# A hybrid decoder layer on one core: the out-projection's weight sums moved to GpSimd's DMA queue, the input projection's sums spread over half blocks

## The chip, the cores and the metric

The kernel runs on one core of one Trainium2 chip. The metric is device time in microseconds (us) of one execution. A core has five engines with a queue each: TensorE (PE; its weight loads are PEld), VectorE (DVE), ScalarE (ACT), GpSimd (POOL) and SyncE (SP, which here only issues DMAs). An engine works through its queue in order. DMAs are issued from SP, from ACT and, after the change, from GpSimd. L12 is line 12 of the kernel before.

## What is computed

One layer of a decoder: a norm, one input projection, three token mixers, one output projection, a residual, a final norm. Cut to that:

```python
h = rms_norm(x, norm_w)
proj = h @ w_in                     # 528 tokens x 2048, all heads of all mixers
o_dn  = gated_delta_rule_chunked(q, k, v, log_a, beta) # 6 heads x 128, gate z
o_gla = gla_chunked(q, k, v, log_g)                    # 5 heads, gate z
o_fox = forgetting_attention(q, k, v, log_f)           # 5 heads x 128, gate z
o = concat([o_dn, o_gla, o_fox])
out = rms_norm(x + o @ w_out)
```

All in fp32, with 512 tokens of sequence and 16 learned ones ahead of them.

## The kernel before, in words

**Products.** Each fp32 operand is split into two parts: `hi`, a rounded copy made by ScalarE (L155), and `lo`, the rest, subtracted by VectorE (L156). A product is three matmuls (hi x hi, hi x lo, lo x hi). The input projection goes by blocks of 128 columns, in two half blocks of weights, each a DMA of 128x1024 on SP into `raw`, one of two buffers (`load_half`, L145), then the split into `whi` and `wlo`, then matmuls into banks `pp`. A load waits until the half block two before it has been split.

**Order of the work.** Delta-rule heads in two groups of three (`g` = 0 and 1): blocks for keys, values and queries, then a matrix inverse that runs mostly on VectorE (`dn_inverse`), whose result TensorE takes up in `pm` (L739), then the chunk recurrence (`dn_mix`). Then five gated-linear heads, five forgetting-attention heads (`fox_head`, numbered 0 to 4, from about 590 to 890 us), and the output projection from about 840 us on. A scheduler that simulates the timeline orders the instructions of each engine, so the projection's matmuls of one head stand between the attention of the head before. Scores (`pfa`, `pfd`) need k scaled by `rstd` on GpSimd (L1117), the transposes `pvf` need v scaled there (L1125), and the gate needs z scaled there (L1127).

**Products saved by sums.** Two places use fewer block products (Strassen's form), and need sums of weights. Both keep the sums in DRAM and read them back as weights.

- *Pairs of the input projection* (`in_sums`, L421): from head 1's v and z on, two blocks are projected together (`inproj_pair`; matmuls L516, casts and splits of halves of 512 columns, loads L504). For each of seven pairs there are four loads of 128x512 (L427, tile `is`), four subtractions or additions on VectorE (L429) and four stores to `ti` (L428), all DMAs on SP. Each sum is tied (`paced`) behind the split that was issued last.
- *The output projection* (`weight_sums`, L588): for each of four pairs of heads `j` and two halves, four loads of 128x512 (L593) into the thirds of one tile `ws`, four subtractions on VectorE (L595), four stores to `tw` (L594). The fourth load writes into a third that the second store reads, so it waits for that store's landing. The tile is one of eight buffers (`six`) which the attention uses too.

**Where the sums are called.** `AHEAD` names the sums that are called at a place of the main loop, `SUMS` those inside `fox_head(h)` behind its projection. Pairs 0 to 2 are called behind the keys, values and queries of group 0, pairs 3 to 6 behind the keys, values, queries and the inverse of group 1. Eight calls of `weight_sums(j, half)` lie in heads 1 to 3.

Of the kernel before, what the change touches and what calls it, by code (L numbers as in the profile page):

```python
# [83 lines left out]
def tile_hybrid_trunk(ctx, tc, xT, xtok, mtok, w_gate, w_in, w_out, w_dn, consts, lmask, fin_w, out, dbg=None):  # L84
    nc = tc.nc
# [13 lines left out]
    def row(name, dt=F32):  # L99
        return wk.tile([P, 3 + T], dt, tag="row", bufs=7, name=name)  # L100
# [44 lines left out]
    def load_half(src, name):  # L145
        raw = wp.tile([P, 1024], F32, tag="raw", name=f"raw{name}")
        nc.sync.dma_start(out=raw, in_=src)
        hi = wp.tile([P, 1024], F32R, tag="hi", name=f"whi{name}")
        lo = wp.tile([P, 1024], F32R, tag="lo", name=f"wlo{name}")
        split(raw, hi, lo)  # L150
        return hi, lo

    def split(raw, hi, lo):
        with tc.high_priority(offset=1000000):
            pace[0] = A.copy(hi, raw).ins  # L155
            pace[1] = V.tensor_tensor(out=lo, in0=raw, in1=hi.bitcast(F32), op=ALU.subtract).ins  # L156
# [3 lines left out]
    def paced(*ins):  # L160

        for x in ins:
            tc.add_manual_dep(x.ins, pace[x.ins.engine == pace[1].engine].name, mybir.DependencyInfo(
                mybir.DependencyClass.NoSync, mybir.DependencyReason.DATA), reason="paced")
# [11 lines left out]
    def part(name, n=512):  # L176
        return hp.tile([P, T], F32R, tag="x", name=name)[:, :n]
# [48 lines left out]
    def inproj(key, meta=True, first=0):  # L226
        if key not in done:
            b, ps, parts = inproj_begin(key, meta, first)
            head[key] = len(order)
            for half in range(2):  # L230
                inproj_part(ps, parts, 8 * half, 8, *load_half(w_in[b, half], f"{b}_{half}"))
            done[key] = [(p_[:, :n], t0, n) for p_, (t0, n) in zip(ps, parts)]
        return done.pop(key)
# [61 lines left out]
    for b in range(5):  # L295
        r = NM if b == 4 else P
        for c in range(2):
            t = wp.tile([P, 1024], F32, tag=("raw", "hi", "lo")[(2 * b + c) % 3], name=f"xt{b}{c}")
# [7 lines left out]
    for b in range(5):  # L306
# [3 lines left out]
        o = pr[1][:, :NM] if b == 4 else pr[0][:, b * P : (b + 1) * P]  # L310
# [24 lines left out]
    def silu(dst, src, name):  # L335
        n = src.shape[-1]
        t = row(f"st{name}")[:, :T]
        t = t[:, :n]
        G.tensor_scalar_max(t, src, LOW)  # L339
        A.activation(t, t, AF.Exp, scale=-1.0)  # L340
        A.activation(t, t, AF.Ln, bias=1.0)
        A.activation(t, t, AF.Exp, scale=-1.0)
        V.tensor_tensor(out=dst, in0=src, in1=t, op=ALU.mult)
# [3 lines left out]
    def gate_z(kind, h, t=None):  # L347
        parts = inproj((kind, h), meta=False)
        p_, t0, n = parts[0]
        z = row(f"z{kind}{h}")[:, :T]  # L350
        V.tensor_tensor(out=z[:, :S], in0=p_, in1=rstd[:, t0 : t0 + n], op=ALU.mult)  # L351
        if t is None:
            t = zp.tile([P, T], F32, tag="zs", name=f"zs{kind}{h}")[:, :S]
        silu(t, z[:, :S], f"{kind}{h}")
        zs[kind, h] = t
# [65 lines left out]
    def stage(name):  # L421
        return [zp.tile([P, T], F32, tag="zs", name=f"{name}{i}")[:, :512] for i in range(3)]

    def in_sums(n):
        h, one, two = PAIRS[n]
        x, y, z = stage(f"is{n}")
        get = lambda o, key, half: nc.sync.dma_start(out=o, in_=w_in[BLOCK_OF[key, h], half][:, :KC])  # L427
        put = lambda i, t: nc.sync.dma_start(out=ti[n][:, i], in_=t)  # L428
        two_ = lambda o, a, b, op: paced(V.tensor_tensor(out=o, in0=a, in1=b, op=op))  # L429
        get(x, two, 0)  # L430
        get(y, two, 1)
        get(z, one, 0)
        two_(y, x, y, ALU.add)
        two_(x, z, x, ALU.subtract)
        put(0, y)
        two_(z, y, z, ALU.subtract)
        put(2, x)
        put(1, z)
        get(x, one, 1)
        two_(x, x, z, ALU.subtract)  # L440
        put(3, x)

# [29 lines left out]
    def x_last(last):  # L472

        f = lambda u: u[:, HT:].bitcast(F32)
        for k in range(NK):
            if not last:
                if k % 2 == 0:
                    t = row(f"xe{k}")
                xr[k] = a = t[:, HT * (k % 2) : HT * (k % 2) + HT]
                V.tensor_tensor(out=a, in0=f(xh[k + 8]), in1=f(xh[k]), op=ALU.subtract)  # L480
                V.tensor_tensor(out=a, in0=a, in1=f(xl[k + 8]), op=ALU.add)
                V.tensor_tensor(out=a, in0=a, in1=f(xl[k]), op=ALU.subtract)
            else:
                A.copy(xh[k][:, HT:], xr[k])
                V.tensor_tensor(out=xl[k][:, HT:], in0=xr[k], in1=f(xh[k]), op=ALU.subtract)
# [101 lines left out]
    tw = drp.tile([SH // 2, 4, P, 1024], F32, name="tw")  # L587

    def weight_sums(j, half):
        c = slice(512 * half, 512 * half + 512)  # L590
        w = six.tile([P, 3, 512], F32, tag="six", name=f"ws{j}{half}")
        x, y, z = (w[:, i] for i in range(3))
        get = lambda o, i, J: nc.sync.dma_start(out=o, in_=w_dn[J, 2 * j + i][:, c])  # L593
        put = lambda n, t: nc.sync.dma_start(out=tw[j, n][:, c], in_=t)  # L594
        sub = lambda o, a, b: V.tensor_tensor(out=o, in0=a, in1=b, op=ALU.subtract)  # L595
        get(x, 0, 1)
        get(y, 0, 0)
        get(z, 1, 1)
        sub(y, x, y)
        sub(x, z, x)  # L600
        sub(z, z, y)
        put(0, y)
        put(2, x)
        put(1, z)
        get(x, 1, 0)
        sub(x, x, z)
        put(3, x)
# [175 lines left out]
    def dn_values(g, st):  # L783
        vp = six.tile([P, NN, P], F32, tag="six", name=f"vp{g}")
        vpm = t15(f"vpm{g}", (NM, H, P))
        br = st["br"]
        for j in range(H):
            h = H * g + j
            v = row(f"v{h}")[:, :T]
            conv_silu(("dv", h), 12 + h, v)  # L790
            pv = psm.tile([P, 512], F32, tag="m", name=f"pv{h}")
            for b in range(NB):
                PE.transpose(pv[:, b * P : (b + 1) * P], v[:, bsl(b)], ident)
            for b in range(NB):
                V.tensor_scalar_mul(vp[:, b * H + j, :], pv[:, b * P : (b + 1) * P], br[:, b, j : j + 1])
            pv2 = psm.tile([P, 512], F32, tag="m", name=f"pvm{h}")
            PE.transpose(pv2[:NM, :P], v[:, 0:NM], ident)
            V.tensor_scalar_mul(vpm[:, j, :], pv2[:NM, :P], br[:NM, 4, j : j + 1])
        st.update(vp=vp, vpm=vpm)

    def dn_queries(g, st):
        qT = six.tile([P, H, T], F32, tag="six", name=f"qT{g}")
        for j in range(H):
            conv_silu(("dq", H * g + j), H * g + j, qT[:, j], meta=False)
        st["qT"] = qT
# [273 lines left out]
    def fox_head(h):  # L1079
# [64 lines left out]
        if h == H1 - 1:  # L1144
            x_sums(XSUM.get(9, ()))
            x_last(False)
        if h in SUMS:
            for j, half in SUMS[h]:
                weight_sums(j, half)
# [47 lines left out]
        V.tensor_tensor(out=z, in0=po[:, :512], in1=z, op=ALU.mult)  # L1197


    SUMS = {1:[(0,1)],2:[(1,1),(3,0)],3:[(2,1),(3,1)]}  # L1200
    XLAST = 0
    AHEAD = {(0,0):(0,),(0,1):(1,),(0,2):(2,),(1,0):(3,),(1,1):(4,),(1,2):(5,),(1,3):(6,),("f",1):((0,0),),("f",2):((1,0),),("f",3):((2,0),)}
    XSUM = {1: (0,), 2: (1,2), 9:(3,)}
    PM = (308, 319)

    def ahead(g, i):
        for n in AHEAD.get((g, i), ()):
            weight_sums(*n) if isinstance(n, tuple) else in_sums(n)

    for g in range(2):  # L1210
        for h in range(max(NF, H * g), H * g + H):
            gate_z("dz", h)
        st = dn_keys(g)
        ahead(g, 0)
        dn_values(g, st)
        ahead(g, 1)
        dn_queries(g, st)
        ahead(g, 2)
        dn_inverse(g, st)
        ahead(g, 3)  # L1220
        dn_mix(g, st)
        for h in range(H * g, H * g + H):
            nc.sync.dma_start(out=zd[h], in_=zs["dz", h])
    for h in range(GLA_HEADS):
        gate_z("gz", h)
    for h in range(DN_HEADS):
# [22 lines left out]
    for mm, n in later:  # L1249
        n = head[n[0]] + n[1] if isinstance(n, tuple) else n  # L1250
        tc.add_manual_dep(mm, order[n].name, mybir.DependencyInfo(
            mybir.DependencyClass.NoSync, mybir.DependencyReason.DATA), reason="behind")


    for i in range(SH):
# [154 lines left out]
    for c in range(4):  # L1410
        f = part(f"fw{c}").bitcast(F32)
# [20 lines left out]
    for tb in range(4):  # L1432
        cuts = 2 if tb == 3 else 1
        for n in range(cuts):
            c = slice(512 // cuts * n, 512 // cuts * (n + 1))
# [79 lines left out]
```

## Time and profile before

| | us |
|---|---|
| median of 3 runs (1021.37 to 1025.98) | 1022.04 |
| the profiled execution | 1020.76 |
| its span, first to last instruction | 1019.0 |
| TensorE busy | 992.3 |
| VectorE busy | 674.8 |
| ScalarE busy | 460.9 |
| GpSimd busy | 195.2 |

The span is shorter than the execution's own time by what lies around it. The granted clock of TensorE is 0.996 over the span. The views name a group of instructions by line, engine, operation and tile (`out<-in`); a wait is read "who <- for whom: us in total, times, longest". A line of the view by stretches has the length, then busy us and (in brackets) the number of instructions of PE, PEld, DVE, ACT and POOL, the granted clock, the DMA engines' busy share and GB/s. Matmuls are pipelined and their ends are modelled, so busy TensorE isn't TensorE at its peak.

### The profile page before, as it was taken

The numbers are of one execution on the slowest core, as the hardware profiler recorded it, in microseconds if no ns is written. First come the engines' busy times: TensorE is split into PE (matmuls) and PEld (weight loads), VectorE is DVE, ScalarE is ACT, GpSimd is POOL, SyncE is SP. The second block draws the span as 40 slices with busy tenths as digits, with TensorE's granted clock in tenths as the row PEclk, the third lists the DMA queues.
The fourth block names the chain that finished last, engine by engine and source line by source line (L and its number), as shares of the span: only waits on it lengthen the run. The fifth ranks groups of instructions, "written<-read, shape, count | busy, mean of one in ns | idle before, by whom it ended". The sixth has DMA issues, their size and how long they took to land.

```text
span 1019.0 us, 19951 instructions
## 1 busy us (share of the span) xinstructions
PE 992.3 (97%) x7866; PEld 907.2 (89%) x7866; DVE 674.8 (66%) x1449; ACT 460.9 (45%) x1041; POOL 195.2 (19%) x192
## 2 busy tenths in 40 slices
PE   9999999999999998999999999989999999999996
PEld 7899999899999787899989978879989998888885
DVE  6367878967676995244666674878475777667673
ACT  7653533334455344244445553435434454444454
POOL 0021411221111331101132620320202114000060
PEclk9999999999999999999999999999999999999999
DMA  9645254345435323122312221466386775456534
GB/s 353 230 140 192 70 154 151 129 140 172 141 103 197 99 87 96 66 83 71 114 60 73 85 73 62 131 209 222 125 259 208 249 254 178 150 180 225 178 114 166
DMA packets 68546, 152.57 MB, mean 150 GB/s; under 512 B 13437, under 2 KB 16685, under 8 KB 68452
## 3 DMA queue, kind: packets, MB, share of 16 engines
q1 hardware_dynamic: 54192, 139.69, 40.0%
q10 hardware_dynamic: 14260, 11.61, 4.2%
q8 instruction: 62, 1.02, 0.4%
q14 instruction: 32, 0.26, 0.1%
HBM read 128.26 MB, written 22.87 MB: 148 GB/s over the span
## 4 chain that ended last, share of the span: by engine, by line
PE 79%; DMA 8%; DVE 7%; ACT 2%; issue 1%; POOL 1%; SPq 1%; ACTq 0%; DVEq 0%; POOLq 0%
PE pp L212 39%; PE pa L1294 5%; PE pp L266 4%; PE pq L1294 4%; PE pt L1294 4%; PE pp_a L516 3%; DMA ws<-in_w_dn 3%; PE ps L1294 2%; DVE wlo L156 2%; PE pp_c L516 2%; PE pp_b L516 2%; PE pp_d L516 1%; DMA raw<-in_w_in 1%; POOL stgz L339 1%; PE pss L987 1%
## 5 line engine op out<-in xcount | busy, mean ns | idle before, releaser
L212 PE MATMUL pp<-xl,whi 128*128 128x264 f32 (+2 forms) x1120 | 285.1, 307 | 0.0
L212 PE MATMUL pp<-xh,whi 128*128 128x264 f32 (+2 forms) x1120 | 283.4, 306 | 0.8 <-DVE fqk L330 0.8
L212 PE MATMUL pp<-xh,wlo 128*128 128x264 f32 (+2 forms) x1120 | 282.9, 306 | 0.6 <-DVE wlo L156 0.6
L155 ACT CAST whi<-raw 128x1024 fp32r<-128x1024 f32 (+1 forms) x159 | 130.1, 840 | 179.3 <-PE pp L212 112.9
L156 DVE TENSOR_TENSOR wlo<-raw,whi 128x1024 fp32r<-128x1024 f32 (+1 forms) x159 | 153.9, 982 | 81.9 <-ACT whi L155 75.7
L212 PEld LDWEIGHTS pp<-xh,whi 128*128 128x128 f32 x1120 | 186.9, 189 | 10.6 <-DVE fqk L330 1.0
L212 PEld LDWEIGHTS pp<-xh,wlo 128*128 128x128 f32 x1120 | 187.0, 189 | 9.8 <-DVE wlo L156 1.0
L212 PEld LDWEIGHTS pp<-xl,whi 128*128 128x128 f32 x1120 | 187.4, 189 | 8.9 <-issue 0.2
L339 POOL TENSOR_SCALAR stc<-cv 128x528 f32<-128x528 f32 (+1 forms) x18 | 29.3, 1628 | 146.9 <-DVE cv L581 120.3
L581 DVE SCALAR_TENSOR_TENSOR cv<-pb,cpk,cv 128x528 f32<-128x528 f32 (+1 forms) x54 | 40.7, 754 | 0.4
L595 DVE TENSOR_TENSOR ws<-ws 128x512 f32<-128x512 f32 x32 | 24.1, 753 | 17.2 <-DMA ws<-in_w_dn 17.1
L516 PE MATMUL pp_a<-xh,whi 128*128 128x264 f32 (+1 forms) x112 | 28.6, 287 | 2.6 <-DVE fqk L541 1.9
L1318 POOL TENSOR_TENSOR acc<-acc,fw 128x512 f32<-128x512 f32 x4 | 6.3, 1594 | 126.5 <-ACT sqf L1315 126.5
L1294 PE MATMUL pa<-whio,ol 128*128 128x512 f32 x72 | 28.4, 395 | 0.0
L155 ACT CAST whis<-raws 128x1024 fp32r<-128x1024 f32 x16 | 16.4, 1047 | 26.6 <-DMA raws<-tw 6.8
L1294 PE MATMUL pa<-wloo,oh 128*128 128x512 f32 x72 | 28.4, 394 | 0.0
L516 PE MATMUL pp_a<-xl,whi 128*128 128x264 f32 (+1 forms) x112 | 28.0, 281 | 0.0
L429 DVE TENSOR_TENSOR is<-is,is 128x512 f32<-128x512 f32 x28 | 19.2, 695 | 12.4 <-DMA is<-in_w_in 12.4
L156 DVE TENSOR_TENSOR wlos<-raws,whis 128x1024 fp32r<-128x1024 f32 x16 | 19.3, 1222 | 10.8 <-ACT whis L155 10.6
L1294 PE MATMUL pa<-whio,oh 128*128 128x512 f32 x72 | 25.9, 400 | 0.0
L516 PEld LDWEIGHTS pp_a<-xh,whi 128*128 128x128 f32 x112 | 21.1, 188 | 3.3 <-ACT whi L155 1.8
L339 POOL TENSOR_SCALAR stdz<-zdz 128x512 f32<-128x512 f32 x6 | 11.2, 1882 | 64.9 <-DVE zdz L351 63.9
(493 smaller groups left out, 2178.1 us busy)
## 6 DMA issues: line engine op xcount, KB each, us to landing
raw<-in_w_in SPq DMA_DIRECT2D x96, 512.0 KB, 3.3
ws<-in_w_dn SPq DMA_DIRECT2D x32, 256.0 KB, 4.5
tw<-ws SPq DMA_DIRECT2D x32, 256.0 KB, 3.8
is<-in_w_in SPq DMA_DIRECT2D x28, 256.0 KB, 4.7
ti<-is SPq DMA_DIRECT2D x28, 256.0 KB, 3.9
raw<-ti SPq DMA_DIRECT2D x14, 512.0 KB, 4.8
rawo<-in_w_out SPq DMA_DIRECT2D x13, 512.0 KB, 4.8
raws<-tw SPq DMA_DIRECT2D x12, 512.0 KB, 4.6
```

Source lines behind the costliest of these rows:

```text
L155: pace[0] = A.copy(hi, raw).ins
L156: pace[1] = V.tensor_tensor(out=lo, in0=raw, in1=hi.bitcast(F32), op=ALU.subtract).ins
L212: mm = PE.matmul(p_[:, :nt], wt[:, j * m : (j + 1) * m], xx[k][:, t0 : t0 + nt], start=(k == 0 and wt is hi and xx is xh), stop=(k == KT - ...
L266: mm = PE.matmul(ps[:, :S], wt[:, j * P : (j + 1) * P], xx[k][:, NM:T], start=(k == 0 and wt is hi and xx is xh), stop=(k == KT - 1 and wt ...
L339: G.tensor_scalar_max(t, src, LOW)
L429: two_ = lambda o, a, b, op: paced(V.tensor_tensor(out=o, in0=a, in1=b, op=op))
L516: m = PE.matmul(p_[:, cols], wt[:, j * P : (j + 1) * P], xx[j][part_][:, cols], start=first and i == 0, stop=last and i == len(todo) - 1, ...
L581: V.scalar_tensor_tensor(out=c, in0=pb[:, t0 + w : w + T], scalar=cwc[:, blk, w : w + 1], in1=c, op0=ALU.mult, op1=ALU.add)
L595: sub = lambda o, a, b: V.tensor_tensor(out=o, in0=a, in1=b, op=ALU.subtract)
L987: mm = PE.matmul(ps[o0 : o0 + n, b * n : b * n + n], kx[rr, k0 : k0 + n], qx[rr, q0 : q0 + n], start=True, stop=True)
L1294: PE.matmul(p_, o_[:, s], w_, start=(first and n == 0), stop=(last and n == 2), skip_group_check=True)
L1318: G.tensor_tensor(out=acc[tb, cc], in0=acc[tb, cc], in1=fw[cc], op=ALU.mult)
```

## The change

It has two parts.

1. The loads and stores of `weight_sums` are issued from GpSimd's queue instead of SP's, and most of the eight calls come later: tile (0,1) moves from head 1 to head 2, (1,1) and (3,0) from head 2's end to ahead of head 3, (0,0) and (1,0) from ahead of a head to its end; (2,0) comes a head earlier.
2. `in_sums` becomes a generator with four stops. All seven pairs are queued (`chores`) ahead of group 0's keys, and each call of `load_half` takes the first of them one step further, behind the split of its half block.

```diff
@@ load_half
         split(raw, hi, lo)
+        for _ in range(rate[0]):
+            if chores:
+                next(chores[0], None) or chores.pop(0)
         return hi, lo
+    chores, rate = [], [1]
@@ in_sums
         get(z, one, 0)
+        yield 1
         two_(y, x, y, ALU.add)
+        yield 1
         two_(x, z, x, ALU.subtract)
         put(0, y)
+        yield 1
         two_(z, y, z, ALU.subtract)
         put(2, x)
         put(1, z)
         get(x, one, 1)
+        yield 1
         two_(x, x, z, ALU.subtract)
         put(3, x)
@@ weight_sums
-        get = lambda o, i, J: nc.sync.dma_start(out=o, in_=w_dn[J, 2 * j + i][:, c])
-        put = lambda n, t: nc.sync.dma_start(out=tw[j, n][:, c], in_=t)
+        get = lambda o, i, J: nc.gpsimd.dma_start(out=o, in_=w_dn[J, 2 * j + i][:, c])
+        put = lambda n, t: nc.gpsimd.dma_start(out=tw[j, n][:, c], in_=t)
@@ the main loop
-    SUMS = {1:[(0,1)],2:[(1,1),(3,0)],3:[(2,1),(3,1)]}
+    SUMS = {1:[(0,0)],2:[(0,1),(1,0)],3:[(2,1),(3,1)]}
-    AHEAD = {(0,0):(0,),(0,1):(1,),(0,2):(2,),(1,0):(3,),(1,1):(4,),(1,2):(5,),(1,3):(6,),("f",1):((0,0),),("f",2):((1,0),),("f",3):((2,0),)}
+    AHEAD = {(0,-1):(0,1,2,3,4,5,6),('f',2):((2,0),),('f',3):((1,1),(3,0))}
     def ahead(g, i):
         for n in AHEAD.get((g, i), ()):
-            weight_sums(*n) if isinstance(n, tuple) else in_sums(n)
+            if isinstance(n, float):
+                rate[0] = int(n)
+            elif isinstance(n, tuple):
+                weight_sums(*n)
+            else:
+                chores.append(in_sums(n))
+        ahead(g, -1)
         st = dn_keys(g)
```

Instructions move on several engines. In the rows below a name carries its numbers (`raw52_1` is part 1 of the weights of block 52, `ws11` the sums of pair 1, half 1, `fqk3` k and q of head 3), and lines of the changed kernel are 6 to 10 higher.

The SP queue before, in the stretch where head 3's projection is loaded and head 2's attention runs:

```order
L504 DMA raw51_5_9172<-in_w_in 128x512 x2
L593 DMA ws11_8866<-in_w_dn 128x512 x3
L593 DMA ws30_8879<-in_w_dn 128x512 x3
L594 DMA tw_708<-ws11_8866 128x512 x3
L594 DMA tw_708<-ws30_8879 128x512
L593 DMA ws11_8866<-in_w_dn 128x512
L504 DMA raw51_6_9217<-in_w_in 128x512
L504 DMA raw52_1_9255<-in_w_in 128x2x512
L594 DMA tw_708<-ws30_8879 128x512 x2
L594 DMA tw_708<-ws11_8866 128x512
L504 DMA raw52_2_9289<-ti_706 128x1024
L593 DMA ws30_8879<-in_w_dn 128x512
```

The SP queue now, at the same place:

```order
L514 DMA raw51_5_9172<-in_w_in 128x512 x2
L514 DMA raw51_6_9217<-in_w_in 128x512
L514 DMA raw52_1_9255<-in_w_in 128x2x512
L514 DMA raw52_2_9289<-ti_706 128x1024
L514 DMA raw52_3_9324<-in_w_in 128x2x512
```

Between the loads of weights stood stores that wait for subtractions and loads that wait for stores; now weights follow weights. GpSimd's queue now, from behind the scaling of head 3's k to the scaling of its v (before, the AFFINE_SELECT alone stood between the two):

```order
L604 DMA tw_708<-ws10_8866 128x512
L604 DMA tw_708<-ws01_8853 128x512
L603 DMA ws10_8866<-in_w_dn 128x512
L603 DMA ws11_8984<-in_w_dn 128x512 x3
L603 DMA ws30_8997<-in_w_dn 128x512 x3
L604 DMA tw_708<-ws10_8866 128x512
L604 DMA tw_708<-ws11_8984 128x512 x3
L604 DMA tw_708<-ws30_8997 128x512 x2
L603 DMA ws11_8984<-in_w_dn 128x512
L604 DMA tw_708<-ws30_8997 128x512
L1147 AFFINE_SELECT fc3_9512<-fc3_9512 128x512
L1135 TENSOR_TENSOR vf3_9251<-vf3_9251,rstd_106 128x528
```

Eight loads and nine stores came in between. VectorE before, where head 2's gate is done and the first subtraction of a group comes:

```order
L343 TENSOR_TENSOR fc2_8853<-zfz2_8593,stfz2_8854 128x512
L549 TENSOR_TENSOR fqk3_8864<-pp51_b_9011,fqk3_8864 128x264
L595 TENSOR_TENSOR ws11_8866<-ws11_8866 128x512
L1164 ISA fp21_8920,fsm21_8921<-pfa21_8916,fc2_8853 128x144
L1164 ISA fsm21_8921 128x1
```

VectorE now, at the same place:

```order
L349 TENSOR_TENSOR fc2_8840<-zfz2_8580,stfz2_8841 128x512
L559 TENSOR_TENSOR fqk3_8851<-pp51_b_9011,fqk3_8851 128x264
L1174 ISA fp21_8907,fsm21_8908<-pfa21_8903,fc2_8840 128x144
L1174 ISA fsm21_8908 128x1
L1191 TENSOR_TENSOR fplo2_8883<-pfx20_8899,fphi2_8882 128x128
L1176 ISA fp21_8907,fsm21_8908<-pfd21_8904,fc2_8840,fsm21_8908 128x128
L1176 ISA fsm21_8908 128x1
L1178 TENSOR_SCALAR fsm21_8908<-fsm21_8908 128x1
L605 TENSOR_TENSOR ws01_8853<-ws01_8853 128x512
```

The first subtraction stands six instructions later. VectorE before, at blocks 23 and 24, ahead of group 1's inverse (`is51` is part 1 of pair 5):

```order
L156 TENSOR_TENSOR wlo23_1_4094<-raw23_1_4091,whi23_1_4093 128x1024
L429 TENSOR_TENSOR is51_4159<-is50_4158,is51_4159 128x512
L429 TENSOR_TENSOR is61_4414<-is60_4413,is61_4414 128x512
L581 SCALAR_TENSOR_TENSOR cv4_4023<-pb4_3910,cpk_97,cv4_4023 128x512
L429 TENSOR_TENSOR is50_4158<-is52_4160,is50_4158 128x512
L429 TENSOR_TENSOR is60_4413<-is62_4415,is60_4413 128x512
```

VectorE now, at the same split:

```order
L162 TENSOR_TENSOR wlo23_1_4124<-raw23_1_4121,whi23_1_4123 128x1024
L591 SCALAR_TENSOR_TENSOR cv4_4053<-pb4_3940,cpk_97,cv4_4053 128x512 x3
L886 TENSOR_TENSOR ff0_2363<-ff0_2363,soo0_2362 128x3
L888 TENSOR_TENSOR ff0_2363<-ff0_2363 128x3
L162 TENSOR_TENSOR wlo24_0_4734<-raw24_0_4731,whi24_0_4733 128x1024
```

Pairs 5 and 6 have left this place, eight subtractions in all with four that stood further on; the last one now stands behind the split of `wlo21_0`.

More of the change, by code (lines that the diff above doesn't have):

```diff
@@ L1223, in tile_hybrid_trunk @@
             nc.sync.dma_start(out=zd[h], in_=zs["dz", h])
+    ahead("gz", 0)
     for h in range(GLA_HEADS):
@@ L1252, in tile_hybrid_trunk @@
             mybir.DependencyClass.NoSync, mybir.DependencyReason.DATA), reason="behind")
+    while chores:
+        next(chores[0], None) or chores.pop(0)
     for i in range(SH):
```

## The prediction

> **What bounds the kernel now.** The first two parts of the page come first: busy time by engine, then the chain of work that ended last.
>
> ```profile
> PE 992.3 (97%) x7866; PEld 907.2 (89%) x7866; DVE 674.8 (66%) x1449; ACT 460.9 (45%) x1041; POOL 195.2 (19%) x192
> PE 79%; DMA 8%; DVE 7%; ACT 2%; issue 1%; POOL 1%; SPq 1%; ACTq 0%; DVEq 0%; POOLq 0%
> ```
>
> TensorE is busy for 992.3 of 1019.0 us, so 26.7 us is all that a better order can win while the matmuls stay the same. The chain leaves TensorE for a fifth of the span, with DMA first. The next view, busy time by stretches, says where.
>
> ```profile
> 60.00:220.00 160.00, 160.00 (x1244) 155.36 (x1243) 126.44 (x274) 64.14 (x122) 32.25 (x34) 1.00 0.44 146
> ...
> 320.00:440.00 120.00, 115.97 (x828) 99.67 (x827) 76.55 (x191) 44.96 (x101) 30.74 (x25) 0.99 0.32 104
> 440.00:640.00 200.00, 197.09 (x2285) 181.53 (x2285) 115.90 (x251) 92.88 (x265) 46.46 (x40) 1.00 0.23 78
> 640.00:700.00 60.00, 54.45 (x403) 51.04 (x403) 46.81 (x121) 27.68 (x68) 14.34 (x17) 1.00 0.57 180
> 700.00:740.00 40.00, 40.00 (x326) 39.41 (x325) 24.96 (x61) 19.10 (x44) 7.75 (x7) 1.00 0.49 162
> 740.00:820.00 80.00, 74.91 (x598) 72.80 (x598) 54.29 (x134) 32.61 (x75) 9.96 (x9) 1.00 0.71 236
> 820.00:840.00 20.00, 20.00 (x157) 19.47 (x156) 13.46 (x25) 11.32 (x24) 3.08 (x3) 1.00 0.81 265
> 840.00:1000.00 160.00, 160.00 (x707) 130.23 (x707) 110.46 (x183) 69.46 (x124) 28.91 (x24) 1.00 0.48 165
> ```
>
> The third column is TensorE's busy time. Between 60 and 220 us, and again after 820, it has no idle time. It lacks 4.0 us in 320 to 440, and 5.6 and 5.1 us in 640 to 700 and 740 to 820, the stretches in which the weight sums run. Who ended TensorE's waits there is the next view (who waited for whom, 640 to 840 us):
>
> ```profile
> PE pp_a L516 <- DVE fqk L541: 1.9, 2, 1.6
> PE pp_b L516 <- ACT whi L155: 1.8, 1, 1.8
> PE pp_a L516 <- ACT fqk L558: 1.5, 1, 1.5
> PE pp_b L516 <- DVE wlo L156: 1.1, 1, 1.1
> PE pp_d L516 <- DVE wlo L156: 1.0, 1, 1.0
> PE pp_d L516 <- ACT whi L155: 1.0, 2, 0.6
> PE pfx L1177 <- DVE fmt L1172: 0.8, 2, 0.6
> PE pfo L1194 <- ACT fp L1183: 0.8, 1, 0.8
> PE pp_a L516 <- DVE fsm L1168: 0.7, 1, 0.7
> ```
>
> That is 10.6 us. No single operation is to blame: casts (L155), splits (L156) and evictions come late together. What holds them is in the view of the tile ws and in the waits of VectorE and of the SP queue:
>
> ```profile
> L593 SPq DMA_DIRECT2D ws<-in_w_dn x32: 332/425/514, 656.2 to 811.0; - x32
>   DMA ws<-in_w_dn: 17.1, 10
> DMA to landing us min/median/max: 2.1/4.3/6.4
> ...
> SPq L594 <- DVE ws L595: 20.8, 15, 3.4
> SPq L593 <- DMA tw<-ws: 11.1, 6, 2.2
> ```
>
> VectorE stood still 17.1 us for landings of ws. The SP queue stood 20.8 us at stores (L594) whose subtraction had not run, and 11.1 us at loads (L593) into a third that was still being stored, with the next load of weights behind them. One of the 10.6 us, the 1.1 of pp_b behind wlo, is the one wait on a split that could be older than the first load of ws at 656.2 us. I leave it out: 9.5 us.
>
> The order of time shows one group of each kind, first VectorE's, then the SP queue's.
>
> ```profile
> 743.96 0.69 DVE L595 TENSOR_TENSOR ws<-ws 128x512 f32<-128x512 f32 x1 [3.06 <-DMA ws<-in_w_dn]
> 744.57 0.30 DVE L1164 CUSTOM_DVE_ANT_0 fp<-pfa,fc 128x144 f32<-128x144 f32 x1
> ...
> 738.18 2.88 SPq L593 DMA_DIRECT2D ws<-in_w_dn  x6
> ...
> 756.42 3.51 SPq L593 DMA_DIRECT2D ws<-in_w_dn  x4
> 759.98 0.43 SPq L504 DMA_DIRECT2D raw<-in_w_in  x1
> ```
>
> Six loads take 2.88 us to issue, VectorE reaches the first subtraction 3.06 us too early, and a load of weights goes out at 759.98, only after four loads of ws that took 3.51 us.
>
> **The change part by part.** *Transfers in GpSimd's queue.* It takes 32 loads and 32 stores off SP. The order keeps SP to weights alone, so the two SP waits above cannot delay a cast any more. On VectorE the first subtraction of the group of heads 2 and 3 stands behind six more instructions of the running head. The longest of them are like the 0.30 us one above, so it comes up to 1.8 us later, and the landing has that much more time. I expect two thirds of the 9.5 us to go: 6.3 us. The ends are 0 (the landings stay late and VectorE waits as before) and 9.5.
>
> What it adds is 64 issues on GpSimd, which the trace of before does not show there. The nearest rows are SP's issue, 0.425 us, and, on GpSimd itself, whole operations:
>
> ```profile
> L1125 POOL TENSOR_TENSOR vf<-vf,rstd 128x528 f32<-128x528 f32 x4 | 6.4, 1602 | 37.4 <-DVE vf L560 36.0 <-ACT fqk L558 1.4
> ...
> L1152 POOL CAST ptm<-zero_c 128x512 fp32r<-128x512 f32 x4 | 3.5, 884 | 0.9 <-PE pfo L1193 0.9
> ```
>
> From 0.43 to 1.6 us each; I take 0.88, the cast of one 128x512 tile on that engine, 56 us in all. GpSimd's busy time from 640 to 840 is 14.34 + 7.75 + 9.96 + 3.08 = 35.1 us, so it would be 91 of 200: hidden, as long as nothing that TensorE needs stands behind a transfer that waits. What stands behind is the scaling of k, v and z by rstd. The tightest is v, which TensorE transposes:
>
> ```profile
> 751.46 1.70 POOL L1117 TENSOR_TENSOR fqk<-fqk,rstd 128x528 f32<-128x528 f32 x1 [14.49 <-DVE fqk L560]
> ...
> 777.78 1.70 POOL L1125 TENSOR_TENSOR vf<-vf,rstd 128x528 f32<-128x528 f32 x1 [5.43 <-DVE vf L560]
> ...
> 785.95 0.60 PE L1089 MATMUL pvf<-ident,vf 128*128 128x128 f32 x4
> ```
>
> From 779.48 to 785.95 it has 6.5 us to spare. In the new order of head 3 eight loads and nine stores stand between the scaling of k and that of v. At 0.88 us they are 15.0 us; two of the loads wait for a store's landing, 2 x 4.3 by the row above: 23.6 us. From 753.16, the end of k's, to 777.78 there are 24.6. So it fits, by 1 us and the 6.5 to spare, if none of the subtractions that the stores wait for is late. I charge 1 us in all for it, with ends 0 and 3 heads x 4.3 = 12.9.
>
> [...] VectorE's scalings of the probabilities run in the same stretch:
>
> ```profile
> L1174 DVE TENSOR_SCALAR fp<-fp,fsm 128x128 f32<-128x128 f32 (+3 forms) x16 | 6.1, 382 | 0.0
> ```
>
> They hold VectorE for 6.1 of 200 us. [...]
>
> *Mostly a head later.* The same bytes move. Head 1 issues one tile instead of two, head 2 three, as before, head 3 four instead of three. The sums are read back only in the output projection, and TensorE has no idle time from 820 to 1000, so the later end costs nothing. More bytes in head 3 are inside the 0 of the lower end.
>
> *The pairs' sums one subtraction behind each half block.* The 28 subtractions, 28 loads and 28 stores stay, the queues too. They now spread from the first convolution block to block 21 and end three blocks earlier. The rows that this touches:
>
> ```profile
> DVE is L429 <- DMA is<-in_w_in: 12.4, 6, 3.1
> ...
> PE pm L739 <- DVE iv L733: 3.0, 1, 3.0
> ```
>
> VectorE's 12.4 us of waits cost TensorE nothing from 60 to 220 us (160.00 of 160.00). Behind 320 us they stand ahead of the second inverse, which runs on VectorE, and TensorE waits 3.0 us for its end. The order takes eight subtractions, at the 0.7 us or so of a 128x512 one (0.69 in the timeline row above) 5.5 us, out of VectorE just ahead of that chain. But the chain's own last steps stand one behind where they were in relation to the splits. Ends 0 and the 4.0 us that TensorE lacks from 320 to 440; I take half of the 3.0: 1.5. The first subtraction comes three half blocks earlier and may wait for its load, at most the 3.1 us seen, under weights that are already split: nothing, since such waits cost nothing there before.
>
> The sum: -6.3 - 1.5 + 1.0 = -6.8 us. The profiled execution took 1020.76 us (span 1019.0, 1.76 around it), so 1013.96. It lies 1.28 below the median of 1022.04, so I forecast 1015.2.
>
> **The rivals.** *No change* (between 1017 and 1027). The subtractions still need their bytes on the same DMA engines, which were busy for 0.71 of 740 to 820, and VectorE still meets them in order; what was waited for behind SP is waited for behind GpSimd. Then only the 1.5 us of the inverse and a third of the 6.3 remain, less 1.0 for v: 1022.0 - 2.6 = 1019.4. For it: the order places each subtraction behind its landing by an assumed landing time, and the 17.1 us show that assumption failing ten times. Against it: the 31.9 us of SP waits are gone in any case. [...]
>
> *Slower: GpSimd is too slow an issuer.* If one issue costs p, the six loads of a group take 6p instead of 2.88 us. The 1.8 us that the six instructions give are used up by a group's last load from p = 0.78 us on (6p - 2.88) and by its second, for which the first subtraction waits, from 1.4 (2p - 0.96). Between them, at about 1.1, the waits are what they were, and above it they grow. At p = 1.6 the last tile of a group lands 6.7 us later, in the three groups of heads 1 to 3: 20 us of VectorE's waits, of which TensorE loses 9.5/17.1, as now: +11. With the inverse's gain of 1.5 and 1 for v that is 1022.0 + 10.7 = 1032.7. The same slow issues use up the 6.5 us of v. For it: GpSimd's own operations lie between 0.88 and 1.6 us. Against it: an issue touches no data, and SP's takes 0.425.
>
> **How the numbers follow.** A difference of about 0.5%, 5.1 us, is what a measurement of this kernel can tell from none. The forecast case (1008 to 1017) gets 0.57, no change (1017 to 1027) 0.28, slower (beyond 1027) 0.15. The best that the bounds allow is 9.5 + 4.0 = 13.5 us, 1008.5. Leaving out the slower case and the upper end of no change is 2 in 10, so the range is 1008 to 1024. The forecast case alone reaches from 1008 to 1017.
>
> **What would show it.** Right: VectorE's waits for ws fall from 17.1 us to under 8, no wait of the SP queue names ws or tw, TensorE's idle time in 640 to 820 falls from 10.6 to about 4, and pm's wait is under 2 us. GpSimd's busy time grows by about 56 us, and the transposes of v never wait for GpSimd. Wrong: issues of over 1 us on GpSimd with VectorE's waits for ws at 17 us or more; TensorE waiting for vf, or for anything of GpSimd's; or idle time in 60 to 220 us, behind a subtraction of the pairs.

## The result, and the profile after

| | before | after |
|---|---|---|
| median, 13 executions each (us) | 1021.17 (1017.02 to 1025.98) | 1016.04 (1011.90 to 1020.62) |
| ratio to before, 95% interval | 1 | 0.9950 (0.9927 to 0.9973) |
| the profiled execution | 1020.76 | 1013.97 |
| its span | 1019.0 | 1012.2 |

The change wins 5.1 us in the medians and 6.8 us between the two profiled executions. Forecast were 1015.2 and -6.8. The total came out; its parts did not all do so. One execution of this case, of `loads_gp` below, took 1380.09 us at a granted clock of 0.653, and its ratio leaves it out.

The busy time by engine on the page of after:

```profile
PE 991.9 (98%) x7866; PEld 908.4 (90%) x7866; DVE 679.6 (67%) x1449; ACT 460.3 (45%) x1041; POOL 225.7 (22%) x256
```

TensorE's busy time is nearly what it was (992.3), so all but 0.4 of the 6.8 us are idle time of TensorE. The view by stretches says where it went (third column: TensorE's busy time). First comes the one stretch of before that the prediction does not show, then those of after:

```profile
220.00:320.00 100.00, 99.90 (x981) 98.31 (x980) 69.31 (x149) 49.20 (x130) 14.86 (x16) 1.00 0.43 139
...
220.00:320.00 100.00, 98.09 (x965) 96.48 (x964) 63.55 (x136) 46.65 (x123) 16.61 (x17) 1.00 0.38 112
320.00:440.00 120.00, 118.67 (x853) 102.84 (x852) 75.78 (x191) 46.68 (x108) 27.99 (x24) 0.99 0.30 93
440.00:640.00 200.00, 198.45 (x2287) 182.40 (x2286) 118.14 (x253) 94.65 (x268) 47.29 (x42) 1.00 0.24 77
640.00:700.00 60.00, 57.78 (x449) 55.62 (x448) 49.15 (x131) 29.25 (x73) 21.92 (x30) 1.00 0.54 169
...
740.00:820.00 80.00, 76.30 (x602) 74.45 (x600) 57.67 (x134) 30.90 (x72) 31.42 (x50) 0.98 0.82 270
```

From 700 to 740 TensorE has no idle time, as before. Length less busy time, against the same stretches of before: 640 to 820 lost 5.9 us instead of 10.6 (-4.7), 320 to 440 1.3 instead of 4.0 (-2.7), 440 to 640 1.5 instead of 2.9 (-1.4), and 220 to 320, which had lost 0.1, now loses 1.9 (+1.8). The sum is -7.0; 0.2 is lost anew behind 820.

TensorE's waits from 640 to 840 us, all that the view names (who waited for whom: us in total, times, longest):

```profile
PE pfx L1187 <- DVE fp L1184: 3.3, 2, 3.0
PE pp_b L526 <- DVE wlo L162: 1.1, 1, 1.1
PE pp_a L526 <- ACT fqk L568: 1.0, 1, 1.0
PE pp_b L526 <- ACT whi L161: 0.2, 1, 0.2
PE pfo L1203 <- ACT fphi L1190: 0.2, 1, 0.2
PE pfd L1171 <- DVE fsm L1174: 0.2, 1, 0.2
```

The crowd of waits on casts, splits and evictions has become one wait of 3.0 us and a few crumbs. None is on GpSimd. The 1.1 us of `pp_b` behind `wlo`, which the prediction left out, is still there. The tile ws, the waits of VectorE for ws and for the pairs' sums, of GpSimd, and of `pm`:

```profile
L603 POOL DMA_DIRECT2D ws<-in_w_dn x32: 536/542/773, 666.2 to 806.1; - x32
DMA to landing us min/median/max: 2.3/4.9/8.6
...
DVE ws L605 <- DMA ws<-in_w_dn: 10.9, 9, 3.7
POOL tw L604 <- DVE ws L605: 43.9, 18, 6.1
DVE is L435 <- DMA is<-in_w_in: 2.1, 2, 1.4
PE pm L749 <- DVE iv L743: 3.2, 2, 1.9
```

The waits at stores have moved with the stores: what SP had as 20.8 us, GpSimd has as 43.9 (with the stores' waits that the view puts down to other instructions of VectorE, 46 and 54). SP's waits in this stretch no longer name ws or tw. An issue takes GpSimd 0.54 us, at most 0.77. The row "DMA to landing" counts the loads and the stores of ws together.

The one long wait that is left can be followed in the order of time, VectorE first:

```profile
762.53 0.69 DVE L605 TENSOR_TENSOR ws<-ws 128x512 f32<-128x512 f32 x1 [3.67 <-DMA ws<-in_w_dn]
763.14 0.68 DVE L162 TENSOR_TENSOR wlo<-raw,whi 128x512 fp32r<-128x512 f32 x1
...
764.08 0.48 DVE L1184 TENSOR_SCALAR fp<-fp,fsm 128x512 f32<-128x512 f32 x1
...
764.71 0.63 PE L1187 MATMUL pfx<-ident,fp 128*128 128x128 f32 x4 [3.02 <-DVE fp L1184]
```

A subtraction whose load had not landed held VectorE for 3.67 us, with a split and the softmax's scaling behind it, and TensorE needed the scaled probabilities. It is the mechanism of before; of nine waits for ws this one alone went through to TensorE in one piece. The DMA engines were busy for 0.82 of this stretch, against 0.71 before.

That wait costs more than its 3.0 us. After, in stretches of 1 us, with the granted clock third from the end:

```profile
763.00:764.00 1.00, 0.00 (x0) 0.00 (x0) 0.96 (x4) 0.37 (x1) 0.48 (x1) 1.00 1.05 424
764.00:765.00 1.00, 0.29 (x3) 0.32 (x4) 1.00 (x3) 0.24 (x1) 0.07 (x1) 1.00 0.88 340
765.00:766.00 1.00, 1.00 (x9) 1.00 (x7) 1.00 (x4) 0.68 (x2) 0.54 (x1) 0.64 0.97 324
766.00:767.00 1.00, 1.00 (x6) 1.00 (x6) 0.96 (x3) 0.32 (x1) 0.46 (x1) 0.50 0.94 346
767.00:768.00 1.00, 1.00 (x7) 1.00 (x6) 1.00 (x2) 0.73 (x3) 0.75 (x3) 0.50 0.65 238
768.00:769.00 1.00, 1.00 (x7) 1.00 (x7) 1.00 (x3) 0.67 (x3) 0.42 (x1) 0.65 1.09 283
```

Behind the wait the clock is halved: 0.36 + 0.50 + 0.50 + 0.35 = 1.7 us are lost, in time that counts as busy. The kernel before has the same behind its 3.0 us wait at the second inverse:

```profile
404.00:405.00 1.00, 1.00 (x5) 0.77 (x4) 0.00 (x0) 0.98 (x2) 0.00 (x0) 0.61 0.00 0
405.00:406.00 1.00, 1.00 (x4) 0.81 (x3) 0.61 (x1) 0.97 (x3) 0.00 (x0) 0.50 0.00 0
406.00:407.00 1.00, 1.00 (x4) 0.72 (x4) 0.61 (x1) 0.22 (x1) 0.00 (x0) 0.50 0.00 0
407.00:408.00 1.00, 1.00 (x5) 0.83 (x4) 0.00 (x0) 0.00 (x0) 0.00 (x0) 0.69 0.37 66
```

Again 1.7 us. In every trace of this case each place between 60 and 1000 us where the clock falls loses 1.7 us or two or three times that: one place of 1.7 in before, two in after, single places of 3.4 and 5.1 us in kernels below. Waits of TensorE from 1.3 us (`pm` in after, at 402 us) to 3.2 us (`pm` in q_only) stood ahead of such drops, and not each wait of that length had one behind it (`pm` waits 1.9 us at the first inverse in after without one, in `chores_only` with one).

### The profile page after: what moved, and what is told of

Its sections match the earlier page's. It is cut to its first block, busy times and chain, and to the rows that moved or that the text cites. A ratio compares the mean times of both kernels' runs of the same rounds, so it can differ in the third digit from the quotient of the medians.

```text
span 1012.2 us, 19962 instructions
## 1 busy us (share of the span) xinstructions
PE 991.9 (98%) x7866; PEld 908.4 (90%) x7866; DVE 679.6 (67%) x1449; ACT 460.3 (45%) x1041; POOL 225.7 (22%) x256
## 4 chain that ended last, share of the span: by engine, by line
PE 81%; DMA 7%; DVE 4%; issue 3%; POOL 3%; ACT 1%; ACTq 0%; POOLq 0%; DVEq 0%
PE pp L218 42%; PE pa L1314 5%; PE pq L1314 4%; PE pp L272 4%; PE pt L1314 4%; PE pp_a L526 2%; PE ps L1314 2%; DMA tw<-ws 2%; DMA ws<-in_w_dn 2%; PE pp_d L526 1%; PE pp_c L526 1%; DVE wlo L162 1%; PE pr L1314 1%; PE pss L997 1%; DMA sc<-ab 1%
## 5 line engine op out<-in xcount | busy, mean ns | idle before, releaser
L162 DVE TENSOR_TENSOR wlo<-raw,whi 128x1024 fp32r<-128x1024 f32 (+1 forms) x159 | 158.3, 1009 | 80.4 <-ACT whi L161 72.2
L605 DVE TENSOR_TENSOR ws<-ws 128x512 f32<-128x512 f32 x32 | 24.0, 753 | 11.0 <-DMA ws<-in_w_dn 10.9
L604 POOL DMA_DIRECT2D tw<-ws x32 | 17.7, 554 | 53.7 <-DVE ws L605 43.9
L852 POOL TENSOR_TENSOR eg<-eg,qT 128x384 f32<-128x384 f32 x8 | 8.1, 1013 | 77.3 <-DVE egl L851 38.7
```

The source lines that it names most:

```text
L604: put = lambda n, t: nc.gpsimd.dma_start(out=tw[j, n][:, c], in_=t)
L852: G.tensor_tensor(out=eg, in0=eg, in1=qT[:, :, ts], op=ALU.mult)
```

## The experiments

Two theories stood behind the forecast: that the queue pays (either because SP no longer waits at stores, or because the loads of the sums no longer share a queue with those of the weights, B where an expectation uses the letter), and against it that the placement, the pairs' sums or a mere reordering of VectorE does. Every edit below is made to the kernel before, and the scheduler orders each kernel anew, so no edit changes a queue alone: against the trace of before some 100 of VectorE's 1449 instructions stand at another place in its order in q_only, as many in loads_gp, some 50 in stores_gp and some 70 in act_queue. "Lost to the clock" is the sum of one less the granted clock over stretches of 1 us from 60 to 1000; "idle" is TensorE's from 640 to 820. Each set of four ran beside its own executions of before, with medians of 1022.25 (33), 1019.27 (26) and 1021.49 (20).

| kernel | median us | ratio (95%) | idle | lost to the clock | VectorE's waits for ws |
|---|---|---|---|---|---|
| before | | 1 | 10.6 | 1.7 | 17.1 |
| after | 1016.04 | 0.9950 (0.9927 to 0.9973) | 5.9 | 3.4 | 10.9 |
| q_only | 1013.78 | 0.9922 (0.9897 to 0.9947) | 7.1 | 3.4 | 8.4 |
| queue_place | 1014.69 | 0.9936 (0.9914 to 0.9957) | 5.2 | 1.7 | 11.5 |
| chores_only | 1020.84 | 0.9987 (0.9965 to 1.0009) | 10.0 | 1.7 | 15.3 |
| place_chores | 1022.01 | 1.0012 (0.9991 to 1.0032) | 11.5 | 3.4 | 19.6 |
| stores_gp | 1022.83 | 1.0028 (1.0011 to 1.0045) | 12.3 | 1.7 | 24.4 |
| loads_gp | 1015.98 | 0.9949 (0.9930 to 0.9969) | 6.6 | 1.7 | 12.5 |
| act_queue | 1023.10 | 1.0030 (1.0011 to 1.0049) | 10.1 | 5.1 | 13.9 |
| no_sums | 1008.48 | 0.9890 (0.9867 to 0.9914) | 2.1 | 1.7 | none |
| gla_gp | 1028.51 | 1.0058 (1.0037 to 1.0079) | 6.9 | 10.2 | 13.9 |
| gla_sp | 1040.35 | 1.0173 (1.0147 to 1.0198) | 9.9 | 12.0 | 18.6 |
| gla_pm16 | 1027.51 | 1.0060 (1.0038 to 1.0082) | 6.4 | 8.5 | 10.5 |
| double_issue | 1022.33 | 1.0006 (0.9986 to 1.0025) | 9.3 | 6.8 | none |

### One part alone, or left out

`q_only` is the queue and no other edit:

```diff
-        get = lambda o, i, J: nc.sync.dma_start(out=o, in_=w_dn[J, 2 * j + i][:, c])
-        put = lambda n, t: nc.sync.dma_start(out=tw[j, n][:, c], in_=t)
+        get = lambda o, i, J: nc.gpsimd.dma_start(out=o, in_=w_dn[J, 2 * j + i][:, c])
+        put = lambda n, t: nc.gpsimd.dma_start(out=tw[j, n][:, c], in_=t)
```

> The kernel before with the 64 transfers of the weight sums in GpSimd's queue and nothing else: calls of the sums and the pairs' sums where they were. Theory (the freed SP queue makes the gain in heads 1 to 3): about 4 us faster than before, TensorE's idle time from 640 to 820 us falls from 10.6 to about 6, no wait of the SP queue names ws or tw. Rival (the later placement makes it, since head 1 then has one tile of sums instead of two): within 1 us of before, idle time from 640 to 820 still 9 us or more, with waits of VectorE for ws at 17 us or more.

Its stretch from 640 to 820, and its waits for ws:

```profile
640.00:820.00 180.00, 172.94 (x1349) 167.62 (x1348) 128.73 (x321) 80.21 (x191) 66.83 (x96) 0.99 0.64 206
DVE ws L595 <- DMA ws<-in_w_dn: 8.4, 7, 2.0
```

The queue alone gives a ratio at least as good as the whole change; the intervals overlap, so more is not shown. Its idle time falls by 3.5 us only, and the clock takes 1.7 back: the profiled execution, at 1017.35 us, is 3.6 above the median, so the trace shows less of the gain than the medians do. Its longest wait:

```profile
766.54 1.14 ACT L155 CAST whi<-raw 128x512 fp32r<-128x512 f32 x2 [5.53 <-DMA raw<-ti]
770.07 1.08 PE L1177 MATMUL pfx<-ident,fp 128*128 128x128 f32 x4 [2.92 <-DVE fmt L1172]
```

Here it is not a subtraction that is late. A load of weights that SP issued at 759.28 held a cast for 5.5 us, VectorE waited 3.65 us for the cast and came late to the scaled probabilities. Nothing of the sums stood in SP's queue then; the DMA engines were busy for 0.80 from 759 to 763 us and for 0.92 from 763 to 767.

`queue_place` adds the new places to it:

```diff
-    SUMS = {1:[(0,1)],2:[(1,1),(3,0)],3:[(2,1),(3,1)]}
+    SUMS = {1:[(0,0)],2:[(0,1),(1,0)],3:[(2,1),(3,1)]}
-... ("f",1):((0,0),),("f",2):((1,0),),("f",3):((2,0),)}
+... ('f',2):((2,0),),('f',3):((1,1),(3,0))}
```

> The changed kernel with the pairs' sums put back where they were in the kernel before. Theory (the pairs' sums bring 1.5 us or so through the second inverse): 1 to 2 us slower than the changed kernel, so about 4 us faster than before; idle time of TensorE from 640 to 820 us about 6 as in the changed kernel, from 320 to 440 us back at about 4. Rival (the spread of the pairs' sums makes the whole gain): no faster than before.

0.9936 against 0.9922: the later places do nothing that these runs can tell.

`chores_only` spreads the pairs' sums and leaves queue and places as before (the stops in `in_sums` are as in the change):

```diff
         split(raw, hi, lo)
+        for _ in range(rate[0]):
+            if chores:
+                next(chores[0], None) or chores.pop(0)
-    AHEAD = {(0,0):(0,),(0,1):(1,),(0,2):(2,),(1,0):(3,), ...
+    AHEAD = {(0,-1):(0,1,2,3,4,5,6), ...
```

> The kernel before with the pairs' sums spread over the half blocks and nothing else. Theory: 1 to 2 us faster than before; VectorE's waits for the pairs' loads fall from 12.4 to about 2 us; idle time of TensorE from 320 to 440 us falls from 4.0 to about 1.3, but about 1.9 us come at the first inverse (220 to 320 us); 640 to 820 us stays at about 10.6. Rival (the spread makes the whole gain): 5 us faster.

Its two stretches with the inverses:

```profile
220.00:320.00 100.00, 98.08 (x952) 96.48 (x951) 63.91 (x136) 46.05 (x119) 15.48 (x17) 0.98 0.38 112
320.00:440.00 120.00, 118.68 (x867) 103.32 (x866) 75.78 (x191) 47.32 (x110) 27.97 (x25) 1.00 0.30 93
```

2.7 us less idle time at the second inverse, 1.8 more at the first, whose `pm` now waits 1.9 us, and the 1.7 us at half clock have moved from the one to the other. VectorE's waits for `is` fall from 12.4 to 2.0 us without a trace in the time. The interval holds 1.

`place_chores` has both but leaves the transfers on SP.

> The changed kernel with the weight sums' transfers back in SP's queue, called at their new places. Theory (the queue makes the gain): 4 us slower than the changed kernel, 1 to 2 us faster than before; idle time of TensorE from 640 to 820 us 9 us or more, and the SP queue waits some 30 us for ws and tw. Rival (the later placement makes it): as fast as the changed kernel, 5 us faster than before, idle time from 640 to 820 us about 6.

1.0012: without the queue the change gains nothing.

### Which transfers, and which queue

`stores_gp` moves the stores alone, `loads_gp` the loads alone, `act_queue` both to ScalarE's queue (`nc.scalar`).

```diff
stores_gp
-        put = lambda n, t: nc.sync.dma_start(out=tw[j, n][:, c], in_=t)
+        put = lambda n, t: nc.gpsimd.dma_start(out=tw[j, n][:, c], in_=t)
loads_gp
-        get = lambda o, i, J: nc.sync.dma_start(out=o, in_=w_dn[J, 2 * j + i][:, c])
+        get = lambda o, i, J: nc.gpsimd.dma_start(out=o, in_=w_dn[J, 2 * j + i][:, c])
```

> The kernel before with the 32 stores of the weight sums in GpSimd's queue; the 32 loads stay on SP. Theory A (what holds the loads of weights on SP are stores that wait for VectorE's subtractions, 20.8 us, and the stores' other waits): most of the gain of the queue, 5 us or more faster than before, TensorE's idle time from 640 to 820 us at 7 or less. Theory B (what matters is that the loads of ws go out early, in a queue of their own): the loads on SP still wait for stores (11.1 us) and go out between loads of weights, VectorE's waits for ws stay at 15 us or more, gain 2 us or less.

> The kernel before with the 32 loads of the weight sums in GpSimd's queue; the 32 stores stay on SP and wait there for the subtractions. Theory A: gain 2 us or less, the stores' waits on SP stay near 45 us in all and casts late. Theory B: most of the gain, 5 us or more, VectorE's waits for ws at 9 us or less.

Waits in stores_gp, of SP and of VectorE:

```profile
SPq L593 <- DMA tw<-ws: 21.5, 8, 7.7
DVE ws L595 <- DMA ws<-in_w_dn: 24.4, 13, 4.0
```

Waits in loads_gp, and its stretch:

```profile
SPq L594 <- DVE ws L595: 27.4, 16, 6.1
DVE ws L595 <- DMA ws<-in_w_dn: 12.5, 8, 2.6
...
640.00:820.00 180.00, 173.42 (x1373) 168.51 (x1372) 127.28 (x326) 80.35 (x193) 46.73 (x61) 1.00 0.65 216
```

With the loads gone SP waits at stores longer than before (27.4 against 20.8 us) and the kernel is as fast as after. With the stores gone SP waits at loads for stores' landings (21.5 against 11.1) and it is slower than before by 0.3%. So SP's waits at stores cost nothing here that these runs can tell; the gain comes with moving the loads of ws.

> The kernel before with all 64 transfers in ScalarE's queue, which issues as SP does and also makes the casts of weights. Theory (the gain comes from a queue in which a waiting transfer holds up nothing that TensorE needs soon): stores and loads that wait now hold ScalarE's casts instead, so slower than the kernel with the transfers in GpSimd's queue by 5 us or more, and no faster than before. Rival (any second queue will do, the transfers just have to leave SP): 6 to 8 us faster than before, like GpSimd's.

Waits in act_queue on ScalarE, whose casts stand behind the transfers now:

```profile
ACT fp L1169 <- DMA tw<-ws: 4.3, 1, 4.3
ACT whi L155 <- DMA tw<-ws: 4.1, 1, 4.1
...
665.32 2.22 ACTq L594 DMA_DIRECT2D tw<-ws  x2
667.66 0.62 ACT L155 CAST whi<-raw 128x512 fp32r<-128x512 f32 x1 [3.72 <-DVE fsm L1168]
668.33 0.39 PE L516 MATMUL pp_d<-xh,whi 128*128 128x264 f32 x1 [1.63 <-ACT whi L155]
674.07 2.07 PE L516 MATMUL pp_a<-t,whi 128*128 128x248 f32 x8 [2.79 <-ACT fqk L558]
```

A load that waits for a store's landing holds a cast or an exponential for 4 us; behind these two TensorE's waits are 1.2 us at most. The clock drops elsewhere: 1.7 of the 5.1 us at the second inverse, as before, and 3.4 from 673 us on, behind waits of 1.6 and 2.8 us for ScalarE, the first of them for a cast behind two stores whose issue took 2.2 us. So a second queue does not pay of itself. That it must be one whose engine TensorE doesn't need in those microseconds fits this run, but one run doesn't show it.

### The ceiling

`no_sums` calls no weight sums at all and reads plain weights in their stead, so the out-projection is not the reference's; the matmuls are as many.

```diff
-    SUMS = {1:[(0,1)],2:[(1,1),(3,0)],3:[(2,1),(3,1)]}
+    SUMS = {}
-    product(pa, "s2", lambda j: tw[j, 1], False, True)
+    product(pa, "s2", lambda j: w_dn[0, 2 * j + 1], False, True)
```

> The kernel before without the weight sums of the output projection: no loads, subtractions or stores for them; the output projection reads the plain weights in the sums' place, as many bytes and matmuls. It is the ceiling for any change of where the sums go. If the idle time of heads 1 to 3 is due to the sums: TensorE's idle time from 640 to 820 us falls from 10.6 to 2 or less and the kernel is 9 to 12 us faster. If VectorE's and TensorE's own order leaves waits there: 4 us or more of idle time stay.

1.1% is all that the sums cost before, some 11 us; the change wins half of that.

### Where the DMA engines are idle

`gla_gp` moves the calls into the gated-linear heads and the first attention heads, with the transfers on GpSimd; `gla_sp` has the same places on SP; `gla_pm16` is gla_gp with `pm` 16 matmuls later.

```diff
-    SUMS = {1:[(0,1)],2:[(1,1),(3,0)],3:[(2,1),(3,1)]}
+    SUMS = {0:[(2,0),(2,1)],1:[(3,0)],2:[(3,1)]}
-... ("f",1):((0,0),),("f",2):((1,0),),("f",3):((2,0),)}
+... ("g",0):((0,0),),("g",1):((0,1),(1,0)),("g",2):((1,1),)}
gla_pm16 as well
-    PM = (308, 319)
+    PM = (308, 335)
```

> The kernel before with the weight sums' transfers in GpSimd's queue and the eight calls moved out of the attention heads into the gated-linear heads (440 to 640 us), where the DMA engines are busy for 0.23 of the time and not 0.71. The queue theory (loads of the weights no longer stand behind those of the sums): what is left in 640 to 820 after the queue, 5 to 7 us, is crowding by the sums themselves and goes too; idle 2 to 3 us there, up to 2 us more in 440 to 640, ratio 0.989 to 0.992, near the 0.989 without any sums. The rival (the gain lies in the order that VectorE happens to get, not in queues): no gain over the transfers alone, ratio 0.992 to 0.996, and idle time of 5 us or more in 440 to 640.

> The same place with the transfers on SP as before. If what cost time was weights behind late loads of sums while the DMA engines were busy, then in the gated-linear heads, at 0.23, the queue matters little: idle 640 to 820 2 to 3 us, ratio 0.990 to 0.994, within 0.3% of the same place on GpSimd. If SP's waits for subtractions and landings themselves hold up the weights wherever they are, the waits of 20 to 40 us on SP turn up in 440 to 640 and TensorE's idle time there grows from 2.9 to 6 us or more: ratio 0.995 to 1.000.

Stretches of gla_gp, then of gla_sp:

```profile
440.00:640.00 200.00, 191.02 (x2230) 176.35 (x2229) 121.82 (x258) 87.16 (x254) 61.23 (x70) 0.98 0.35 115
640.00:820.00 180.00, 173.08 (x1319) 167.05 (x1318) 121.47 (x302) 80.52 (x193) 52.06 (x66) 0.97 0.48 156
```

```profile
440.00:640.00 200.00, 186.40 (x2191) 171.88 (x2191) 120.45 (x254) 85.26 (x240) 41.49 (x37) 0.98 0.36 115
640.00:820.00 180.00, 170.08 (x1283) 162.75 (x1284) 111.87 (x284) 79.61 (x196) 34.10 (x34) 0.97 0.46 148
```

Both theories expected a gain or no loss, and both were wrong: with these places the kernel is 0.6% slower than before on the new queue (q_only is 0.8% faster) and 1.7% slower on the old. Idle DMA engines alone were not what the sums lacked. TensorE's waits in gla_gp, 440 to 640:

```profile
PE pss L987 <- DVE kq L973: 2.7, 1, 2.7
PE py L853 <- DVE zz L849: 2.5, 1, 2.5
PE pt L885 <- ACT on L882: 2.3, 1, 2.3
```

The recurrences there take turns between TensorE, VectorE and ScalarE, and have waits of 2 to 3 us that they did not have before. Of the 10.2 us that gla_gp loses to the clock, 3.4 lie behind the waits of `py` and `pss` (at 474 and 573 us), 1.7 at the second inverse as before, and 5.1 from 679 us on in the attention. Ahead of `zz`, which `py` waits for at 474 us, stand three subtractions and a wait of 1.8 us for a landing of ws; ahead of the other two late steps no subtraction stands in the 10 us before, so what delays them stays open. The pair speaks for the queue all the same: with places alike, SP costs 1.1% more than GpSimd, and the intervals are apart, though some 150 instructions of VectorE stand at other places between the two.

> The sums in the gated-linear heads on GpSimd's queue, and TensorE takes up the inverse's result 16 matmuls later. If the 3.0 us wait of pm for iv is only that pm stands too early, it goes and nothing else is late: idle 320 to 440 falls from 3.5 to 1 us, ratio 0.2 to 0.3% below the one without this edit. If the recurrence behind pm is the longer chain, the wait moves to its later steps, and the ratio stays.

1.0060 against 1.0058: no gain. `pm` still waits 3.1 us for `iv`, and idle time from 320 to 440 is 4.8 us instead of 3.3. The wait is not that `pm` stands a few matmuls too early.

### Twice as many issues

`double_issue` is q_only with every transfer in two halves of 256 columns.

```diff
+        def get(o, i, J):
+            for s in (0, 256):
+                nc.gpsimd.dma_start(out=o[:, s : s + 256], in_=w_dn[J, 2 * j + i][:, 512 * half + s : 512 * half + s + 256])
```

> The transfers alone in GpSimd's queue, each split into two of 256 columns: 128 issues, so that a 512-column transfer takes about 1.08 us of GpSimd's time, at which the rival of the slow issuer had the waits back where they were. The queue theory: GpSimd's busy time grows by another 35 us, the subtractions wait some us longer for ws (8.4 with whole transfers, 10 to 14), TensorE's idle time in 640 to 820 stays under 8.5, ratio 0.992 to 0.996. The slow-issuer rival: waits for ws of 17 us or more, idle 10 us or more in 640 to 820, ratio 0.998 to 1.003. Rows of half the length can also make each landing later, which either would show as time to landing above 4.9 us.

The tile ws:

```profile
L595 POOL DMA_DIRECT2D ws<-in_w_dn x64: 536/536/773, 649.9 to 830.2; - x64
DMA to landing us min/median/max: 2.0/3.7/7.3
```

Half the columns take as long to issue, so a 512-column tile costs GpSimd 1.07 us, and the gain is gone: 1.0006. That is the time which the slow-issuer rival gave for 1.1 us. But its mechanism is not there: VectorE does not wait for ws once, and landing is quicker, not later (3.7 against 4.7 us in q_only). The queue theory's forecast (0.992 to 0.996) failed as well: the loads are out of SP's queue, and the gain is not there. The last store goes out at 839 us instead of 817, TensorE waits 5.2 us in all for `fmt` on VectorE and 2.3 us in the out-projection, and loses 6.8 us to the clock. Which of the reordered steps brings this about stays open.

## Why the prediction was right in its total

**The queue, -6.3.** Shown in direction and place; the term was mis-sized. Idle time in 640 to 820 fell by 4.7 of the 10.6 us, not by 6.3 (by 3.5 in q_only), and the last long wait added 1.7 us at half clock. The signs were mixed: SP's waits no longer name ws or tw, as said, but VectorE's waits for ws fell to 10.9 us, where under 8 was forecast, and TensorE's idle time to 5.9, where about 4 was. The step that failed is "the two SP waits cannot delay a cast any more": the larger of the two was no cost that these runs can tell. loads_gp keeps it, at 27.4 us, and gains as much as the whole change. What costs, by the pair loads_gp and stores_gp, is the load of ws in line with the weights. How is argued: the weights stand behind it, and, with 24.4 us of VectorE's waits in stores_gp, it stands behind stores and weights and lands late. The two directions were not taken apart further, and a rival stands: each kernel's order of VectorE shifts as well, in q_only for 25 of the 32 subtractions, and no run holds the order fixed. VectorE's waits for ws are no measure of the gain either: double_issue has none, and no gain.

**The places, 0.** Right: queue_place against q_only, place_chores against chores_only. The four tiles in head 3 raised the DMA engines' share to 0.82, beside the one long wait that is left; q_only, at 0.74 from 740 to 820, has one of 2.9 us too, behind a late load of weights.

**The pairs' sums, -1.5.** 0.9 us net in the trace (-2.7 and +1.8), inside the noise in time. What failed is that the sum priced the second inverse alone. The sums were spread over group 0's blocks as well, VectorE's busy time from 60 to 220 us rose from 126.4 to 134.3 us, and the first inverse, which had no wait, got one of 1.9 us, in chores_only too. That "such waits cost nothing there before" is no answer to it: the waits for loads are down to 2.1 us, and TensorE still has no idle time from 60 to 220. Which step of the first inverse is late was not followed. `pm`'s sign (under 2 us) holds for each of its two waits, 1.9 and 1.3, and not for their sum of 3.2; the clock still dropped behind the second.

**GpSimd, +1.0.** Nothing: no wait of TensorE from 640 to 840 us names it. The issue was priced at 0.88 us by a cast on the same engine; it is 0.54, nearer to the other end, SP's 0.43. So 64 issues take 35 us instead of 56, and GpSimd's busy time grew by 30.5. The 17 issues ahead of the scaling of v are 9.2 us at that price, where 15.0 still fitted.

**Not in the sum.** 1.4 us less idle time in 440 to 640, where a 1.4 us wait of `pss` is gone, and the half clock, which no term priced. The too large terms of queue and inverse (1.6 and 0.6 us) were made good by this 1.4 and by the 1.0 that GpSimd did not cost. That the total met -6.8 to a tenth is luck; in the medians it is -5.1. The 1.7 us more at half clock don't show in the total because busy time is 2.1 us shorter elsewhere; why, no run tells.

**The rivals.** "No change" had this much right: in after the subtractions still wait for late bytes, 10.9 us in all. But it left the queue a third of the 6.3 us, and q_only, the queue alone, is 0.8% faster. That the point is which in-order queue a transfer waits in is what act_queue and the pair of gla kernels speak for, with the orders not held fixed. And the late load of weights in q_only, at a DMA share of up to 0.92, looks like the crowding that this rival spoke of. "Too slow an issuer" was not met at 0.54 us; at twice as many issues its time was met, by another way. The longest of the 64 issues took 0.77 us. Transfers of ws land later (median 4.9 against 4.3 us, longest 8.6 against 6.4); whether the fuller DMA engines (0.82 against 0.71 from 740 to 820) are why, no run shows.

## What to carry to other kernels

Before moving DMAs off a queue, ask of each kind by itself what stands behind it: a store that waits may be harmless where a load ahead of weights is not (0.9949 in loads_gp against 1.0028 in stores_gp), and what the engine of the new queue does for the bottleneck. Where a scheduler reorders with each edit, count how much of the order moved before the queue gets the credit. A place with idle DMA engines was no free place here (1.0058 in gla_gp), where the work also takes turns on the engines of a tight recurrence. Where rows of 1 us show the clock halved behind a wait of TensorE, count that with the wait: it was 1.7 us behind each of the two waits of 3.0 us in before and after.

## What the hardware showed that was not expected

The granted clock over the span goes with the time of an execution: of 79 executions of before, the 23 with a clock of 0.993 or less have a median of 1023.5 us, the 24 with 0.996 or more 1019.1 us. Each drop takes 1.7 us, 0.0017 of the span, so by an estimate from these rows two or three drops more or fewer would make that difference of 4.4 us; the drops were counted in the profiled executions only.

GpSimd's issue takes 0.54 us for 128x512 and for 128x256 alike, SP's 0.43 for loads (before) and 0.32 for stores (loads_gp), ScalarE's 0.36 and 0.33 (act_queue). The landing of ws's transfers, loads and stores together, has a median of 4.7 to 4.9 us behind GpSimd's issue (q_only, after) against 4.3 behind SP's (before, where the trace has 22 of the 64). At the places of the gla kernels it is the other way, 3.6 (gla_gp) against 4.0 (gla_sp), so no rule for the issuer comes out of it.
